# Hybrid decoder trunk on one core: an earlier order for the RWKV stage's chunk products, inversion and small products

## The chip, the core and the metric

The kernel runs on one core of one Trainium2 chip. The time is the device time of one execution in microseconds (us). Below, PE is the TensorE's matmul engine, DVE is VectorE, ACT is ScalarE, POOL is GpSimd and SP the queue that issues the DMAs. The time of the kernel before is 2563.52 us, the median of 3 runs.

## The reference

One layer of a decoder is computed for a prompt of 1024 tokens (plus 16 learned tokens) and for 8 samples of 8 tokens, both with the same weights, all in float32. The core of it:

```python
proj = x @ lw['w_in']
hA, (C1, n1, m1) = _mlstm_mixer(...)      # 4 heads, chunkwise matrix memory
hB, S1, shift1 = _rwkv7_mixer(...)        # 16 heads of 64, delta update of a state
merged = sigmoid(gA) * hA + sigmoid(gB) * hB
x1 = _layer_norm(ALPHA * x + merged @ lw['w_out'], ...)
x2 = _layer_norm(ALPHA * x1 + conv_ffn(x1), ...)

def _rwkv7_step(S, inp):
    r, w, k, v, kk, a = inp
    sa = jnp.einsum('bhvk,bhk->bhv', S, -kk)
    S = S * w[:, :, None, :] + sa[..., None] * (kk * a)[:, :, None, :] + v[..., None] * k[:, :, None, :]
    return S, jnp.einsum('bhvk,bhk->bhv', S, r)
```

The change lies in the RWKV mixer alone. The kernel computes that recurrence in chunks of 64 tokens: within a chunk the updates of the delta rule are a triangular system, whose matrix comes from products of r, a with k, b and is inverted; between chunks a state S is carried on.

## The kernel before, in words

The kernel has two phases. Phase 1 normalises the input, runs the mLSTM mixer and then the RWKV stage (from about 410 us to 1640 us of the profile); phase 2 makes the output product, the second normalisation and the convolution feed-forward. All large products are made of three float32r products of high and low parts (`mm3`, L59), 24 matmuls to a 128-row weight block; eight units of three matmuls make one block, and below a **unit** is such a group of three (`lerp`, L305, and `tanh_gate`, L328, yield after each).

The RWKV stage (`rwkv`, L1141) works on steps 0 to 11: 3 passes over the tokens (346, 384 and 384 columns) by 4 groups u of four heads each (two blocks m of 128 rows). It is a software pipeline. In step n of its loop these things go on side by side:

- the **chain** of step n (`rwkv_chain`, L935): 18 rounds of small float32 matmuls, each needing the one before, which carry the state from chunk to chunk;
- the back part of step n-1 (`rwkv_back`, L1050);
- for step n+2 the dense products of k and r (`rwkv_k`, L672, `rwkv_r`, L693), for step n+1 those of v, and some gate products; these are the units, some 102 to a step in passes 1 and 2, and they fill the time between the chain's rounds;
- for step n+2 the "inside" work (`inner`, L1236): the **chunk products** (`rwkv_g`, L770), then on DVE the **inversion** of the triangular matrices by forward substitution (`rwkv_t`, L823; 30 pairs of DVE instructions, L837 and L839, on the tile LX), then two further products and copies that complete the inverse TT (`rwkv_mid`, L872).

Four kinds of **small products** belong to the dense work: the **rate** products in `rwkv_r` (decay and in-context rate, four matmuls into the tile gg, then two tanh on ACT, L714), the **norm** products in `rwkv_r` (sums of squares over a head; sq, the square, is made by ACT, L728), the **bonus** product (`rwkv_bonus`, L845) and the **gate** product (`gates_b`, L628).

What sets the order: PE's order is the program's own (`manual_schedule`, L1327). The order on DVE, ACT and POOL is made by the framework's scheduler. The loop at L1242 has 18 rounds to a step; in each round it issues one round of the chain, then the back part, then inside work whose due time has come (due times are fractions of a step after the step in which the inside work begins), then its share of the units. Rate and norm products stand in `rwkv_r` in program order between the units; bonus and gate pieces are put in a list and issued by `dense` (L1199) after 6 or 4 units.

The tile gg is two banks of PSUM and exists once (`gbank`, L226): rate products, chunk products and the two products of the completion (`product`, L888) all go through it, so each waits until the one before has been read out. A chunk product is read by two DVE instructions into Gd (L804), an ACT copy into A21 (L810), and two DVE instructions into Gr and Gk (L812, L813). Gd exists once: the chunk products of a step may be read into it only after LX has been taken from it for the step before (L830). `product` issues its first half and, when it is called on again or when `gbank` is, its second half; its results are copied by ACT (L908 for the first, L913 for the second).

Due times before: chunk products from 0.42 of a step on, in steps of 0.075 (0.06 in pass 0, where the samples' chunk is separate), all four or five in one run; the inversion from 0.87 on for 0.75 of a step; completion from 1.78 on. The list `share` (L1167) gives the number of gate products for steps -2, -1, 0, ..., 12.

Of the kernel before, what the change touches and what calls it, by code (L numbers as in the profile page):

```python
# [43 lines left out]
class Trunk:  # L44
# [303 lines left out]
    def lora(self, pas, w, pool):  # L348
        x = self.rs.tile([P, W], F32, name="sq")
# [278 lines left out]
    def gates_b(self, pas, j, w, pool):  # L628
# [18 lines left out]
        self.small += [(self.cfg.get("b1", 4), piece)]  # L647
# [23 lines left out]

    def rwkv_k(self, pas, j, w, pool):  # L672

        nc, i = self.nc, self.i
        m = j % 2
        st = self.st[pas, j] = {}
# [16 lines left out]
    def rwkv_r(self, pas, j, w, pool):  # L693
# [8 lines left out]
        st = self.st[pas, j]  # L702
        r, k, a, b, lw = (st[n] for n in ("r", "k", "a", "b", "lw"))
# [36 lines left out]
        n2 = r_["n2"]  # L740
        ps = self.psc.tile([P, 512], F32, name="y", bufs=2)
        for p in range(NP):
            self.mm(ps[:, 2 * p:2 * p + 2], sq[:, p * 128:(p + 1) * 128], self.const("bones2"))
        c = slice(6 * m, 6 * m + 6)
        ts(n2[:, c].rearrange("p (h n) -> p n h", h=2), ps[:, 0:6].rearrange("p (n h) -> p n h", h=2), 1e-24, None, op0=ALU.max)
# [17 lines left out]
        if m:  # L763
            self.un[pas, j // 2] = dict(n2L=n2L)
# [5 lines left out]
    def rwkv_g(self, pas, u, pool):  # L770
# [6 lines left out]
        done, total = 0, 5 if pas == 0 else 4  # L777
        for m, st in self.pairs(pas, u):
# [44 lines left out]
    def rwkv_t(self, pas, u, pool):  # L823
# [9 lines left out]
        for s in range(1, 31):  # L833
# [6 lines left out]
            if s % 2 == 0:  # L840
                yield self.cfg.get("t0", 0.87) + self.cfg.get("tw", 0.75) * s / 30
# [299 lines left out]
    def rwkv(self, steps):  # L1141
# [567 lines left out]
```

## Time and profile before

| | us |
|---|---|
| median of 3 runs (2560.59 to 2563.93) | 2563.52 |
| the profiled execution's own time | 2555.19 |
| its span, first to last instruction | 2553.4 |
| PE matmul busy in it | 2373.9 (93%) |
| DVE busy | 1546.8 (61%) |
| ACT busy | 1085.0 (42%) |
| POOL busy | 477.0 (19%) |
| mean granted clock of TensorE | 0.964 of full |

Busy shares are means over stages that differ, so the RWKV stage is read from windows of the trace (times from the span's start) and from lists of who waited for whom within it. Granted clock 1.0 is 2.4 GHz and 0.5 is 1.2 GHz. A wait is put down to the releaser that came last.

### The profile page before, as it was taken

Reading aid. Unit: us, or ns where it says so; the run is one execution under the profiler, and the core shown is the slowest. Engines: PE = TensorE matmul, PEld = TensorE weight load, DVE = VectorE, ACT = ScalarE, POOL = GpSimd, SP = SyncE. Lnnn points to the kernel's source line nnn. Section 1 sums busy time; section 2 is a strip of 40 time slices with the busy share of each in tenths; the row PEclk is TensorE's granted clock in tenths of the full one; section 3 lists DMA queues with packets and bytes.
Section 4 is the critical chain, followed back from the end, with each engine's and each line's share of the span. In section 5 each row is a group of like instructions: output and inputs, shape, how many; then the busy total and the mean of one; then the engine's idle time right before and its main releaser. Section 6 shows DMA issues by size and latency. Waiting matters only on the chain. (4 is left out here: it accounts for less than half of the span.)

```text
span 2553.4 us, 43721 instructions
## 1 busy us (share of the span) xinstructions
PE 2373.9 (93%) x16303; PEld 2139.4 (84%) x16303; DVE 1546.8 (61%) x3365; ACT 1085.0 (42%) x2453; POOL 477.0 (19%) x669
## 2 busy tenths in 40 slices
PE   6999998879899899999989999998999999999997
PEld 6787996768787788888878888887999999999996
DVE  6555536888885588765698874456433333343437
ACT  4444444335434456545645655455313222132222
POOL 5100015434553212111111212221000000000003
PEclk9999998889999899999999999989999999999999
DMA  8563534435458355557455566894111111021112
GB/s 281 158 187 93 187 114 138 152 120 176 127 164 257 108 167 162 172 180 252 140 165 160 173 208 215 277 317 167 59 34 54 38 46 50 30 63 34 50 38 81
DMA packets 212362, 356.95 MB, mean 140 GB/s; under 512 B 24610, under 2 KB 83874, under 8 KB 212151
## 3 DMA queue, kind: packets, MB, share of 16 engines
q1 hardware_dynamic: 212151, 354.17, 43.5%
q8 instruction: 128, 2.10, 0.4%
q14 instruction: 83, 0.68, 0.1%
HBM read 272.00 MB, written 82.08 MB: 139 GB/s over the span
## 5 line engine op out<-in xcount | busy, mean ns | idle before, releaser
L57 PE MATMUL d<-Xh,whi 128*128 128x384 f32 (+3 forms) x1544 | 557.5, 361 | 14.7 <-ACT sm L1137 3.9
L57 PE MATMUL d<-Xl,whi 128*128 128x384 f32 (+3 forms) x1544 | 530.8, 344 | 1.2 <-DMA Xl<-xl_d 0.8
L57 PE MATMUL d<-Xh,wlo 128*128 128x384 f32 (+3 forms) x1544 | 528.3, 342 | 0.2 <-DVE wlo L74 0.2
L57 PE MATMUL d<-X1h,whi 128*128 128x364 f32 (+2 forms) x1120 | 371.4, 332 | 4.5 <-ACT whi L90 2.8
L57 PE MATMUL d<-X1h,wlo 128*128 128x364 f32 (+2 forms) x1120 | 370.4, 331 | 0.0
L57 PE MATMUL d<-X1l,whi 128*128 128x364 f32 (+2 forms) x1120 | 370.3, 331 | 0.0
L57 PEld LDWEIGHTS d<-Xh,whi 128*128 128x128 f32 (+1 forms) x1544 | 302.3, 196 | 39.5 <-issue 8.7
L57 PEld LDWEIGHTS d<-Xl,whi 128*128 128x128 f32 (+1 forms) x1544 | 302.8, 196 | 5.7 <-DMA Xl<-xl_d 4.0
L57 PEld LDWEIGHTS d<-Xh,wlo 128*128 128x128 f32 (+1 forms) x1544 | 301.8, 195 | 2.8 <-DVE wlo L74 0.6
L73 ACT CAST whi<-raw 128x512 fp32r<-128x512 f32 (+1 forms) x255 | 157.0, 617 | 339.0 <-PE d L57 277.2
L57 PEld LDWEIGHTS d<-X1h,whi 128*128 128x128 f32 x1120 | 212.1, 189 | 9.5 <-ACT whi L90 3.4
L57 PEld LDWEIGHTS d<-X1l,whi 128*128 128x128 f32 x1120 | 211.9, 189 | 4.9
L57 PEld LDWEIGHTS d<-X1h,wlo 128*128 128x128 f32 x1120 | 212.0, 189 | 3.6 <-DMA wlo<-lo_w_out_b 0.3
L90 ACT CAST whi<-raw 128x512 fp32r<-128x512 f32 x232 | 142.9, 617 | 133.3 <-PE d L57 68.5
L74 POOL TENSOR_TENSOR wlo<-raw,whi 128x512 fp32r<-128x512 f32 x120 | 164.7, 1374 | 181.5 <-ACT whi L73 162.3
L1537 DVE TENSOR_TENSOR acc<-y,acc 128x512 f32<-128x512 f32 (+1 forms) x144 | 97.5, 686 | 166.1 <-PE y L57 166.0
L74 DVE TENSOR_TENSOR wlo<-raw,whi 128x512 fp32r<-128x512 f32 (+1 forms) x135 | 98.6, 734 | 157.6 <-ACT whi L73 156.7
L839 DVE TENSOR_TENSOR LX<-LX,tm 128x30 f32<-128x30 f32 (+4 forms) x360 | 148.0, 411 | 9.8 <-DVE tm L837 0.5
L837 DVE TENSOR_TENSOR tm<-LX 128x30 f32<-128x30 f32 (+4 forms) x360 | 138.6, 385 | 8.8
L57 PE MATMUL y<-wdh,hh 128*128 128x512 f32 x352 | 138.1, 392 | 5.0 <-DVE acc L1537 5.0
L57 PE MATMUL y<-wdl,hh 128*128 128x512 f32 x352 | 137.8, 391 | 0.0
L57 PE MATMUL y<-wdh,hl 128*128 128x512 f32 x352 | 137.6, 391 | 0.0
(363 smaller groups left out, 4175.5 us busy)
## 6 DMA issues: line engine op xcount, KB each, us to landing
raw<-in_w_up_dram SPq DMA_DIRECT2D x88, 256.0 KB, 2.8
raw<-in_wv_dram SPq DMA_DIRECT2D x48, 256.0 KB, 3.1
raw<-in_wk_b_dram SPq DMA_DIRECT2D x48, 256.0 KB, 3.9
raw<-in_wr_dram SPq DMA_DIRECT2D x48, 256.0 KB, 3.2
raw<-in_wv_b_dram SPq DMA_DIRECT2D x48, 256.0 KB, 3.4
raw<-in_wgb_dram SPq DMA_DIRECT2D x48, 256.0 KB, 3.6
raw<-in_wo_dram SPq DMA_DIRECT2D x48, 256.0 KB, 3.6
raw<-in_wga_dram SPq DMA_DIRECT2D x48, 256.0 KB, 3.3
```

Of the source, the lines that this page charges most:

```text
L57: self.nc.tensor.matmul(out, lhsT, rhs, start=start, stop=stop, skip_group_check=skip)
L73: nc.scalar.copy(hi[:, :n], src[:, u:u + n])
L74: self.lo_eng.tensor_tensor(lo[:, :n], src[:, u:u + n], hi[:, :n].bitcast(F32), op=ALU.subtract)
L90: nc.scalar.copy(hi, raw)
L837: tt(tv_, LX[:, s + 1:, s:s + 1].broadcast_to([P, m, s]), LX[:, s:s + 1, 0:s].broadcast_to([P, m, s]), op=ALU.mult)
L839: tt(LX[:, s + 1:, 0:s], LX[:, s + 1:, 0:s], tv_, op=ALU.add)
L1537: tt(acc[0:m, t, ns], ps[0:m], acc[0:m, t, ns], op=ALU.add)
```

## The change

No instruction is added or removed on any engine; all of it is order.

- Rate, norm, bonus and gate products all go into the list `small`, and the loop takes one of them from it in each round, behind the chain's round, the back part and the inside work, ahead of the units. `rwkv_r` puts its rate product there at its start and flushes it before it is needed, after five units; `lora`, `rwkv_r` and the end of a step flush what is left.
- Chunk products are due pair by pair: block m=0 at 0.22, 0.33 of a step, block m=1 at 0.46, 0.57, each as soon as its block's inputs have been issued (`able`), no longer when both have; and not before the step before has begun its inversion (the flag "begun").
- The inversion is due from 0.79 on, and the completion's parts at 1.72, 1.775, 1.83, 1.885 and 1.94, one to a round.
- `share` gives step -1 nine gate products (six before), step 1 five (six) and step 2 four (six).

```diff
@@ -348,0 +349 @@
+        self.flush()
@@ -647 +648 @@
-        self.small += [(self.cfg.get("b1", 4), piece)]
+        self.small.append(piece)
@@ -671,0 +673,5 @@
+    def flush(self, last=None):
+        while self.small and (last is None or last in self.small):
+            self.small.pop(0)()
@@ -675,0 +682,2 @@
+        if not m:
+            self.un[pas, j // 2] = {}
@@ -702,0 +711,2 @@
+        self.flush()
+        self.within = True
@@ -707,9 +717,12 @@
-        zs = self.gbank()
-        for n in range(2):
-            rows = slice(64 * n, 64 * n + 64)
-            x, ps = self.xwa[n], zs[:, n, 0:W]
-            self.mm(ps, lw[0][:, 2 * rows.start:2 * rows.start + 128], x, True, False)
-            self.mm(ps, lw[1][rows], x[rows], False, True)
-        for n, (dst, bias) in enumerate(((cw, dv(3)), (ta, dv(4)))):
-            act(dst, zs[:, n, 0:W], AF.Tanh, bias=bias, scale=0.5)
-        for _ in range(4):
+        def rates():
...
+        self.small.append(rates)
+        for _ in range(5):
@@ -716,0 +730 @@
+        self.flush(rates)
@@ -740,10 +754,13 @@
-        n2 = r_["n2"]
...
-        nc.vector.reciprocal(n2[:, c], n2[:, c])
-        if m:
-            n2L = pool.tile([P, 32], F32, name="n2L", bufs=2)
-            nc.vector.transpose(n2L, n2)
+        def norms():
...
+            if m:
+                n2L = self.un[pas, j // 2]["n2L"] = pool.tile([P, 32], F32, name="n2L", bufs=2)
+                nc.vector.transpose(n2L, n2)
+        self.small.append(norms)
@@ -763,2 +780 @@
-        if m:
-            self.un[pas, j // 2] = dict(n2L=n2L)
+        self.within = False
@@ -777,2 +793,5 @@
-        done, total = 0, 5 if pas == 0 else 4
-        for m, st in self.pairs(pas, u):
+        for m in range(2):
+            un["wait"] = "DL", m
+            yield 0.22 + 0.24 * m
+            done, total = 0, 3 if pas == 0 else 2
+            st = self.st[pas, 2 * u + m]
@@ -815 +834,2 @@
-                    yield self.cfg.get("g0", 0.42) + self.cfg.get("gw", 0.3) * done / total
+                    yield 0.22 + 0.24 * m + 0.22 * done / total
+        un["wait"] = "n2L", None
@@ -829 +849 @@
-        yield self.cfg.get("t0", 0.87)
+        yield self.cfg.get("t0", 0.79)
@@ -830,0 +851 @@
+        self.un[pas, u]["begun"] = True
@@ -843 +864 @@
-        yield self.cfg.get("t0", 0.87) + self.cfg.get("tw", 0.75)
+        yield self.cfg.get("t0", 0.79) + self.cfg.get("tw", 0.75)
@@ -869 +890 @@
-        self.small += [(6, piece)]
+        self.small.append(piece)
@@ -879 +900 @@
-        m0 = self.cfg.get("m0", 1.78) if (pas, u) != (0, 0) else self.cfg.get("m00", 1.78)
+        m0 = self.cfg.get("m0", 1.72) if (pas, u) != (0, 0) else self.cfg.get("m00", 1.72)
@@ -885 +906 @@
-        yield m0 + 0.1
+        yield m0 + 0.055
@@ -908 +929 @@
-        yield from (m0 + 0.12 for _ in product(A21, Tn, 0, 32, lambda w, h1: nc.scalar.copy(P1[h1], w[h1])))
+        yield from (m0 + 0.11 for _ in product(A21, Tn, 0, 32, lambda w, h1: nc.scalar.copy(P1[h1], w[h1])))
@@ -912,2 +933,2 @@
-        yield m0 + 0.15
-        yield from (m0 + 0.17 for _ in product(P1, Tx, 32, 0, lambda w, h0: nc.scalar.copy(
+        yield m0 + 0.165
+        yield from (m0 + 0.22 for _ in product(P1, Tx, 32, 0, lambda w, h0: nc.scalar.copy(
@@ -917 +938 @@
-            yield m0 + 0.2
+            yield m0 + 0.23
@@ -1143 +1164 @@
-        self.st, self.un, self.tho, self.mt, self.rest = {}, {}, {}, {}, None
+        self.st, self.un, self.tho, self.mt, self.rest, self.small, self.within = {}, {}, {}, {}, None, [], False
@@ -1167 +1188 @@
-        share = self.cfg.get("ga", [0] + [6] * 8 + [5, 5, 5, 9, 0, 0])
+        share = self.cfg.get("ga", [0, 9, 6, 5, 4, 6, 6, 6, 6, 5, 5, 5, 9, 0, 0])
@@ -1201,2 +1221,0 @@
-            since = 0
-            self.small = []
@@ -1211,2 +1230 @@
-                    while self.small:
-                        self.small.pop(0)[1]()
+                    self.flush()
@@ -1218,2 +1235,0 @@
-                if not self.small:
-                    since = 0
@@ -1225,6 +1241 @@
-                    since += 1
-                    if self.small and since >= self.small[0][0]:
-                        self.small.pop(0)[1]()
-                        since = 0
-            while self.small:
-                self.small.pop(0)[1]()
+            self.flush()
@@ -1239,0 +1251,7 @@
+        def able(m):
+            pas, u = steps[m]
+            what, which = self.un.get((pas, u), {}).get("wait", ("DL", 0))
+            where = self.un.get((pas, u), ()) if which is None else self.st.get((pas, 2 * u + which), ())
+            return what in where and (m == 0 or "begun" in self.un[steps[m - 1]])
@@ -1246 +1264 @@
-                inside[n + 2] = [0.42, inner(n + 2)]
+                inside[n + 2] = [0.22, inner(n + 2)]
@@ -1256 +1274 @@
-                if r == 12 and 0 <= n + 1 < N:
+                if r >= 12 and 0 <= n + 1 < N and "bon" not in self.st[steps[n + 1][0], 2 * steps[n + 1][1]] and not self.within:
@@ -1264 +1282 @@
-                    while x[0] <= now and "n2L" in self.un.get(steps[m], ()):
+                    while x[0] <= now and able(m):
@@ -1266 +1284 @@
-                        if m in starts and x[0] < self.cfg.get("t0", 0.87):
+                        if m in starts and x[0] < self.cfg.get("t0", 0.79):
@@ -1267,0 +1286,2 @@
+                if self.small:
+                    self.small.pop(0)()
```

What the order becomes, at three places.

PE, in the last rounds of step 8, where products that complete an inverse are issued (T is the inverse so far, A the matrix A21, d the dense products, u, y and t the chain's; a product is issued in two halves). Before, the second half of the first product and the first half of the second follow each other:

```order
L57 MATMUL d<-Xh,wlo 128x384
L57 MATMUL u<-VU,KBT 64x64 x4
L57 MATMUL y<-VU,Gr 64x64 x4
L57 MATMUL gg<-T_16352,A_14800 32x32 x12
L57 MATMUL gg<-T_16350,A_14800 32x32 x12
L57 MATMUL d<-Xh,whi 128x384
```

In the change each half stands in a round of its own, here one half of the second product:

```order
L57 MATMUL d<-Xh,wlo 128x384
L57 MATMUL u<-Rs,TT_4224 64x64 x4
L973 MATMUL t<-cst,v 128x128
L975 MATMUL t<-cst,KB 128x128 x2
L57 MATMUL gg<-T_16241,A_14812 32x32 x12
L57 MATMUL d<-Xh,whi 128x384
```

The two products that stood side by side on gg are now a round of dense units apart.

DVE, step 8: the last products of k and b (KB), then the reading of the first chunk product for step 10 (Gd, Gr, Gk), with n the norms and T the transposed inverse. Before:

```order
L759 TENSOR_TENSOR KB<-KB,ta 128x3x2x64
L1039 SCALAR_TENSOR_TENSOR S_4211<-u,DL,SD 64x64 x4
L1083 SCALAR_TENSOR_TENSOR ysq<-t,pt,bon 128x3x64 x2
L882 STREAM_TRANSPOSE T_16350<-LX 128x1024
L884 STREAM_TRANSPOSE T_16352<-LX 128x1024
L760 TENSOR_TENSOR KB<-KB,sm 128x3x128
L804 TENSOR_TENSOR Gd<-gg,cst 32x6x32 x2
L1083 SCALAR_TENSOR_TENSOR ysq<-t,pt,bon 128x3x64 x2
L323 SCALAR_TENSOR_TENSOR v<-d,pd,sm 128x384
L1092 SCALAR_TENSOR_TENSOR ysq<-ysq,pt,mA 128x384
L812 TENSOR_TENSOR Gr<-gg,cst 128x384
L813 TENSOR_TENSOR Gk<-gg,cst 64x384
```

The change:

```order
L777 TENSOR_TENSOR KB<-KB,sm 128x3x2x64
L860 TENSOR_TENSOR LX<-LX,tm 128x2x29
L858 TENSOR_TENSOR tm<-LX 128x30
L860 TENSOR_TENSOR LX<-LX,tm 128x30
L863 TENSOR_TENSOR LX<-LX,n2L 128x1024
L823 TENSOR_TENSOR Gd<-gg,cst 32x6x32 x2
L903 STREAM_TRANSPOSE T_16241<-LX 128x1024
L905 STREAM_TRANSPOSE T_16243<-LX 128x1024
L760 TENSOR_SCALAR n_4231<-y 128x3x2
L831 TENSOR_TENSOR Gr<-gg,cst 128x384
L832 TENSOR_TENSOR Gk<-gg,cst 64x384
```

Before, the two transposes of LX were over when the first chunk product was read, and that reading came many rows after the products of block m=0; now the last product of block m=0, the end of the inversion and the two transposes stand directly around it.

ACT, step 8: sq and the rates' two tanh (cw, ta). Before:

```order
L321 ACTIVATE sm<-d,pt 128x384
L714 ACTIVATE cw<-gg,pd 128x384
L714 ACTIVATE ta<-gg,pd 128x384
L728 ACTIVATE sq<-KB,pt 128x3x64 x2
L1041 COPY Yt<-y 128x128
```

The change:

```order
L321 ACTIVATE sm<-d,pt 128x384
L742 ACTIVATE sq<-KB,pt 128x3x64 x2
L1062 COPY Yt<-y 128x128
L998 ACTIVATE SD<-S_4211,DL 128x128
L725 ACTIVATE cw<-gg,pd 128x384
L725 ACTIVATE ta<-gg,pd 128x384
```

The squares now stand ahead of the two tanh instead of behind them.

## Rows read from the trace of the kernel before

**Rows 1.** Busy time by stretch: us, PE, PEld, DVE, ACT, POOL busy, clock, DMA share, GB/s.
```profile
440.00:551.00 111.00, 83.12 (x576) 75.06 (x574) 96.69 (x221) 39.12 (x87) 47.40 (x61) 0.83 0.45 141
551.00:755.00 204.00, 180.43 (x1546) 157.84 (x1545) 170.49 (x378) 99.04 (x252) 103.10 (x127) 0.95 0.50 155
755.00:971.00 216.00, 199.07 (x1549) 172.95 (x1548) 146.44 (x321) 105.31 (x259) 49.65 (x81) 0.92 0.55 173
971.00:1339.00 368.00, 348.62 (x2931) 306.37 (x2930) 272.82 (x659) 206.28 (x505) 54.82 (x96) 0.98 0.56 180
1339.00:1640.00 301.00, 289.60 (x2522) 255.87 (x2521) 198.72 (x481) 171.88 (x439) 62.59 (x65) 0.98 0.63 197
```

**Rows 2.** Waits of PE, 440 to 1640, then 440 to 551: total, times, longest.
```profile
PE gg L57 <- DVE Gk L813: 28.3, 15, 3.9
PE gg L57 <- DVE T L884: 17.0, 3, 14.3
PE gg L57 <- ACT A L908: 12.7, 12, 1.1
PE y L57 <- ACT sq L728: 9.9, 2, 5.2
PE y L57 <- POOL T L929: 5.8, 3, 2.8
...
PE gg L57 <- DVE Gk L813: 10.2, 7, 3.0
```

**Rows 3.** Timeline of PE completing one inverse: start, us, [idle before <-releaser].
```profile
1418.01 0.85 PE L57 MATMUL gg<-T,A 32*32 32x32 f32 x24 [1.05 <-ACT A L908]
```

**Rows 4.** Groups of instructions, ACT, the copies behind the second product: busy, mean ns.
```profile
L913 ACT COPY TT<-gg 32x384 f32<-32x384 f32 x24 | 20.1, 837 | 1.0 <-PE gg L57 0.9
```

**Rows 5.** Timeline of ACT, step 0, the squares.
```profile
582.55 0.80 ACT L728 ACTIVATE sq<-KB,pt 128x192 f32<-128x192 f32 x2 [2.66 <-DVE KB L323]
```

**Rows 6.** Timeline of PE, then of DVE, at the first step's inverse.
```profile
525.59 0.87 PE L57 MATMUL gg<-T,A 32*32 32x32 f32 x24 [14.31 <-DVE T L884]
...
523.65 1.89 DVE L884 STREAM_TRANSPOSE T<-LX 128x1024 f32<-128x1024 f32 x1
```

**Rows 7.** Groups of DVE, the reading of chunk products: busy, mean ns.
```profile
L804 DVE TENSOR_TENSOR Gd<-gg,cst 32x192 f32<-32x192 f32 x80 | 40.1, 502 | 16.4 <-PE gg L57 15.2
...
L813 DVE TENSOR_TENSOR Gk<-gg,cst 64x384 f32<-64x384 f32 x40 | 22.0, 549 | 0.3
```

**Rows 8.** Timelines of PE and DVE, step 9, then step 1: rates to last KB product.
```profile
1428.35 0.70 PE L57 MATMUL gg<-xw,lw 128*128 128x384 f32 x2
...
1435.92 0.83 PE L57 MATMUL y<-cst,sq 128*128 128x2 f32 x6
...
1438.38 0.76 PE L57 MATMUL u<-Rs,TT 64*64 64x64 f32 x8
...
1439.04 0.56 DVE L760 TENSOR_TENSOR KB<-KB,sm 128x384 f32<-128x384 f32 x1
...
654.07 0.71 PE L57 MATMUL gg<-xw,lw 128*128 128x384 f32 x2
...
680.71 0.51 DVE L760 TENSOR_TENSOR KB<-KB,sm 128x384 f32<-128x384 f32 x1
```

**Rows 9.** Timeline of PE, dense matmuls of 346 columns at either clock.
```profile
470.33 0.32 PE L57 MATMUL d<-Xl,whi 128*128 128x346 f32 x1
...
470.49 0.33 PE L57 MATMUL d<-Xh,wlo 128*128 128x346 f32 x1
...
485.91 0.49 PE L57 MATMUL d<-Xh,whi 128*128 128x346 f32 x1
...
486.20 0.49 PE L57 MATMUL d<-Xl,whi 128*128 128x346 f32 x1
```

**Rows 10.** Timeline of DVE, then of POOL, step 9.
```profile
1428.36 1.51 DVE L839 TENSOR_TENSOR LX<-LX,tm 128x184 f32<-128x184 f32 x1
...
1428.13 1.53 POOL L1074 TENSOR_TENSOR Yt<-Yt,yvar 128x768 f32<-128x768 f32 x1
```

More of the change, by code (lines that the diff above doesn't have):

```diff
@@ L705, in rwkv_r @@
         units = self.lerp(pas, w, j, mu(0), dv(0), r, pool)
-        zs = self.gbank()
-        for n in range(2):
-            rows = slice(64 * n, 64 * n + 64)
-            x, ps = self.xwa[n], zs[:, n, 0:W]
-            self.mm(ps, lw[0][:, 2 * rows.start:2 * rows.start + 128], x, True, False)
-            self.mm(ps, lw[1][rows], x[rows], False, True)
-        for n, (dst, bias) in enumerate(((cw, dv(3)), (ta, dv(4)))):
-            act(dst, zs[:, n, 0:W], AF.Tanh, bias=bias, scale=0.5)
-        for _ in range(4):
+        def rates():
+            zs = self.gbank()
+            for n in range(2):
+                rows = slice(64 * n, 64 * n + 64)
+                x, ps = self.xwa[n], zs[:, n, 0:W]
+                self.mm(ps, lw[0][:, 2 * rows.start:2 * rows.start + 128], x, True, False)
+                self.mm(ps, lw[1][rows], x[rows], False, True)
+            for n, (dst, bias) in enumerate(((cw, dv(3)), (ta, dv(4)))):
+                act(dst, zs[:, n, 0:W], AF.Tanh, bias=bias, scale=0.5)
+        self.small.append(rates)
+        for _ in range(5):
             yield next(units)
+        self.flush(rates)
         ts(cw, cw, DECAY_C, DECAY_C, op0=ALU.mult, op1=ALU.add)
@@ L738, in rwkv_r @@
         yield from units
-        n2 = r_["n2"]
[L741 to L745, printed above, removed]
-        nc.vector.reciprocal(n2[:, c], n2[:, c])
-        if m:
-            n2L = pool.tile([P, 32], F32, name="n2L", bufs=2)
-            nc.vector.transpose(n2L, n2)
+        def norms():
+            n2 = r_["n2"]
+            ps = self.psc.tile([P, 512], F32, name="y", bufs=2)
+            for p in range(NP):
+                self.mm(ps[:, 2 * p:2 * p + 2], sq[:, p * 128:(p + 1) * 128], self.const("bones2"))
+            c = slice(6 * m, 6 * m + 6)
+            ts(n2[:, c].rearrange("p (h n) -> p n h", h=2), ps[:, 0:6].rearrange("p (n h) -> p n h", h=2), 1e-24, None, op0=ALU.max)
+            nc.vector.reciprocal(n2[:, c], n2[:, c])
+            if m:
+                n2L = self.un[pas, j // 2]["n2L"] = pool.tile([P, 32], F32, name="n2L", bufs=2)
+                nc.vector.transpose(n2L, n2)
+        self.small.append(norms)
         yield
@@ L840, in rwkv_t @@
             if s % 2 == 0:
-                yield self.cfg.get("t0", 0.87) + self.cfg.get("tw", 0.75) * s / 30
+                yield self.cfg.get("t0", 0.79) + self.cfg.get("tw", 0.75) * s / 30
         tt(LX, LX, n2L.unsqueeze(1).broadcast_to([P, 32, 32]), op=ALU.mult)
-        yield self.cfg.get("t0", 0.87) + self.cfg.get("tw", 0.75)
+        yield self.cfg.get("t0", 0.79) + self.cfg.get("tw", 0.75)
     def rwkv_bonus(self, pas, j, pool):
```

## The prediction

> **What bounds the kernel now.** I first read the windows of the RWKV stage [rows 1]. In every stretch from 440 to 1640 us PE is busy far more than any other engine, except in the first, 440 to 551, where PE has 83.1 of 111 us and DVE 96.7. Summed over the five rows PE is busy 1100.8 of 1200 us, so 99 us are idle. The granted clock adds to that: 1 minus the clock, times the length, times two is the time spent at 1.2 GHz: 38, 20, 35, 15 and 12 us, 119 in all, idle time included. What a us at the low level loses is seen in two pairs of equal matmuls, which start 0.16 us apart at one level and 0.29 at the other [rows 9]: 45%. So the stage has two stores from which a new order can draw: idle PE time, and a clock that falls where PE idles (0.92 and 0.95 in the two stretches of pass 0, 0.98 where PE idles about 5%).
>
> Next come the waits of PE [rows 2]. They name gg above all: 28.3 us behind the last reading of a chunk product (15 waits, 10.2 us of it in the seven before 551), 17.0 behind the transposed inverse (one wait of 14.3), 12.7 behind the copy of a product of the completion (12 waits, each about 1.05 [rows 3]), 9.9 behind the squares, 5.8 behind a transpose on POOL in pass 0 (L929). No instruction is added or removed, so all that can change is these waits, new ones like them, and the clock.
>
> **The change part by part.** All terms are us of the profiled execution, 2555.19, which is 8.3 under the median of the runs.
>
> *Completion, spread over rounds.* A copy of 1.05 now lies behind a round's units instead of on the path [rows 3]. Ten of the twelve waits go: -10.5. In two steps (2 and 6, where a pass ends) the order puts the next rates right behind the second product; they then wait for the two copies behind it, 2 x 0.84 [rows 4], in place of nothing: +1.8. Sum -8.7.
>
> *Norm products, a round or more later, and squares ahead of the tanh on ACT.* The two waits over 4 us and what is with them go: -9.9 [rows 2]. A doubt: in step 0 the square itself waited 2.66 us for DVE's KB [rows 5], so a part may stay if DVE is later still.
>
> *POOL's transpose.* The product before it ends some three units earlier. A unit is three matmuls at 0.16, 0.48 [rows 9]; 3 x 0.48 = 1.45 for each of three waits, of which two are longer than that and the third is short: -3.3 of 5.8.
>
> *The first inverse.* PE waits 14.31 us for a transpose that DVE ends at 525.5 [rows 6]; DVE is the bound there [rows 1]. The same instructions stand ahead of it in both orders, so the chunk products of step 1, of which five now come in a run, wait under the same cover and cost nothing by themselves; if the cover were gone they would cost their readings, about 3.5 each. Readings that come in between on DVE push the transposes to between 527 and 533; I take 4 us. The order has 17 more units behind the inverse and ahead of the chain's start (17 x 0.48 = +8.2) and 24 fewer later, in steps 1 and 2 (-11.5), since step -1 got three gate products more. Sum +0.7.
>
> *Readings of chunk products.* Outside the start 28.3 - 10.2 = 18.1 us of waits stand behind them [rows 2]. In most steps each product on gg is now followed by a round of other work, longer than its reading of about 2 x 0.50 + 2 x 0.55 us on DVE [rows 7]. They all go, -18.1, and three new costs are put against them:
>
> 1. **Chunk products wait for their inputs.** In steps 0, 1, 4, 5, 8 and 9 the first product of block m=0 now comes soon after that block's k and b have been made. Between the rates and this product PE has, by the order, the rates (0.70 [rows 8]), about eight units (24 matmuls of 384 columns, 0.18 each by scaling 0.16 from 346: 4.3), the norms (0.83) and two pieces of the chain (about 0.8 to 1.2 each): some 8 us. Before, the last KB of a block was written 11.25 us after its rates began in step 9 (to 1439.6), and 27.1 us after them in step 1 (to 681.2) [rows 8]. From above: 4 x 3.2 in passes 1 and 2, 2 x 18 in pass 0: 49. From below: 0, since the order puts less in between on DVE (in step 8 the k product now directly precedes the inversion's end). I take 2.5 each, nearer the row of step 9, six times: +15.
> 2. **Rates behind chunk products.** In steps 4 and 8 two transposes, 1.89 for the one in [rows 6], now stand between a product's readings. That makes about 5.5 us against some 4.7 of PE's work: 0.7, four times: +2.8.
> 3. **Two products in one round** in steps 3 and 7: the second waits a reading, about 3: +6.
>
> With these the readings come out at +5.7.
>
> As to two products in a row on the one tile, the Trainium skill (Perfetto Trace Analysis, section Optimizing Tensor Performance, Matmuls) says that independent matmul groups should go round different PSUM banks so that the read-out of one overlaps the next; gg is two banks that are used as one, and [rows 2] agree with 28.3 us. By that rule the change would gain wherever it parts such products and pay only in steps 3 and 7 and at the start.
>
> *Clock.* The low level followed waits of some us on PE [rows 1, 2]. With the two waits of about 5 us and some of about 3 gone I take 9 us fewer at 1.2 GHz: 9 x 0.45 = -4. Bounds: 0, and -17 if the 55 us of 551 to 971 came down to the 17 that a clock of 0.98 would make.
>
> **Sum:** -8.7 - 9.9 - 3.3 + 0.7 + 5.7 - 4 = -19.5. The profiled execution would take 2535.7, the median **2544**. About 0.2% (5.1 us) is what a measurement of this kernel can tell from no change.
>
> **The rivals.**
>
> *DVE delivers late (slower).* The place is the first chunk product of block m=0 in the six steps of item 1. DVE is busy 170 of 204 us in steps 0 and 1 [rows 1], and one of its instructions of some 0.4 us took 1.51, beginning 0.2 us after a POOL instruction of 1.53 and ending with it [rows 10]. If such meetings, or the inversion that is now due sooner, keep the last KB as late as it was before, item 1 is at its upper end, 49 instead of 15: 2544 + 34 = **2578**. It decides from 15 + 19.5 = 34.5 us over the six waits, 5.8 each. For it speaks step 1's 27 us; against it that only steps 0 and 1 are so crowded, and that POOL has under 63 us busy in each of the later stretches. A rule of the Trainium skill speaks for it (SBUF - State Buffer, section Who interferes with whom): a DVE instruction with two inputs in SBUF contends with a GpSimd instruction that reads SBUF, and the one that comes second is held off; [rows 10] agree, and the KB products have both inputs there.
>
> *Waits only move (no change).* In pass 0 DVE sets the pace, and what PE gains there it waits for at the next product. Then the norms' 9.9, POOL's 3.3 and the clock's 4 are not gained: -2.3, a median of **2561**. For it speaks the square that itself waited for DVE [rows 5].
>
> *Everything arrives in time (faster still).* Item 1 costs nothing (-15), and the clock gives half of its bound, 8.5 instead of 4 (-4.5): **2524**. Against it stand step 1's 27 us.
>
> That the change moves nothing is excluded by the order itself.
>
> **How the numbers follow.** Forecast 0.45; DVE late 0.22; waits move 0.18; all in time 0.15. The forecast's own bounds (item 1 by 10 either way, the clock by 4) reach from 2533 to 2556. The range leaves out about the outer half of the two extreme rivals: 2514 to 2578. Faster by over 0.2% are the forecast, all in time: 0.60. Waits move lies within 0.2%, less a little that belongs to slower: 0.17. Slower: 0.23.
>
> **What would show it.** Right: PE's waits behind the copy of the first product (A, now L929) fall from 12.7 us to about 3; no wait over 1 us behind the squares; few waits of gg behind Gk (now L832) between 551 and 1640, except one in each of steps 3 and 7; the first wait behind the inverse ends between 527 and 533, and the chain's first step begins some 10 us later than 551 without the end of the stage being later. Item 1 shows as waits of gg behind KB (L777, L778) of about 2.5. The forecast is wrong if these are over 5.8 each, if DVE's busy share in pass 0 is unchanged and PE idles there under other names, or if the clock of 551 to 971 falls below 0.92.

## The result, and the profile after

The change is **slower**: 2592.83 us, the median of 4 runs (2589.52 to 2603.86), against 2563.72 for the kernel before beside it. The ratio is 1.0116, 95% interval 1.0087 to 1.0145. Run again beside other kernels it was 1.0128 (1.0097 to 1.0159). The forecast was 2544, range 2514 to 2578.

The profiled execution took 2603.86 us (span 2601.8), 48.7 more than that of before and itself 11 above its median, so the first thing is to see where those 48.7 us lie. The RWKV stage, taken from the first rate product to the end of the last product with an inverse in a chain (u from Rs and TT), took 1212.3 us before and 1243.3 now: +31. It began 10.1 us later (423.0 after 412.9), and 7.6 us were added behind it. Those two parts belong to the execution more than to the change: in a second profile of the same kernel the stage began at 414.9, and in the profiles of the other kernels below it began anywhere from 411.5 to 425.5. So the 31 us are what has to be explained.

Windows of the change by the same stretches of the program (each ends where the chain of the same step begins; the last ends as far behind the last chain as in [rows 1]). Columns as in [rows 1]:

```profile
440.00:576.00 136.00, 106.44 (x693) 97.77 (x693) 113.01 (x262) 49.80 (x113) 63.45 (x79) 0.82 0.48 155
576.00:781.00 205.00, 183.54 (x1529) 158.89 (x1526) 165.60 (x356) 96.88 (x247) 95.28 (x119) 0.91 0.46 145
781.00:992.00 211.00, 182.93 (x1487) 157.43 (x1485) 151.07 (x337) 101.42 (x249) 45.09 (x79) 0.93 0.52 167
992.00:1376.00 384.00, 356.52 (x2929) 312.87 (x2929) 272.87 (x657) 206.96 (x505) 55.45 (x97) 0.95 0.53 171
1376.00:1681.00 305.00, 294.67 (x2528) 260.99 (x2528) 197.56 (x469) 172.51 (x439) 60.99 (x66) 0.97 0.61 195
```

Against [rows 1] the first stretch is 25 us longer, 10 of them because the stage began later. It has 117 matmuls more, 72 of them the 24 units that the new shares put there. The next two stretches have 79 matmuls fewer and are together only 4 us shorter; the fourth, with the same matmuls but two, is 16 longer. The granted clock is lower in steps 0 and 1 (0.91 after 0.95) and in passes 1 and 2 (0.95 and 0.97 after 0.98). The whole stage, before and in the change:

```profile
412.90:1625.21 1212.31, 1112.63 (x9147) 977.18 (x9147) 895.45 (x2085) 628.75 (x1551) 336.57 (x472) 0.95 0.55 174
...
423.04:1666.30 1243.26, 1126.52 (x9141) 988.75 (x9141) 904.54 (x2085) 629.02 (x1550) 333.24 (x472) 0.93 0.53 169
```

PE's idle time rose from 99.7 to 116.7 us, and the matmuls that started at 1.2 GHz from 463 to 611; PE's busy time is 13.9 us longer for the same instructions but six. 17.0 + 13.9 are the 31 us. How much of the 13.9 is the change's own is less sure than the sum looks: a kernel as fast as the one before (d2 below) had 6 us more PE busy time in its profile than the profile of before. That the clock fell doesn't hang on these profiles: the median granted clock of whole runs was 0.954 in both sets of runs of the change, and 0.962 in the 23 runs of the kernel before beside the second set.

The waits of PE, 440 to 1640 us of the change (total, times, longest):

```profile
PE gg L57 <- DVE T L905: 25.0, 3, 11.4
PE gg L57 <- DVE Gk L832: 19.1, 9, 4.7
PE gg L57 <- DVE KB L777: 18.9, 6, 4.4
PE gg L57 <- DVE S L1054: 10.3, 3, 4.0
PE gg L57 <- DVE T L1035: 7.5, 3, 4.8
PE gg L57 <- DVE LX L860: 6.7, 2, 4.5
PE gg L57 <- DVE tm L858: 4.6, 1, 4.6
PE gg L57 <- ACT TT L934: 3.6, 2, 1.9
...
PE y L57 <- ACT sq L742: 2.0, 1, 2.0
```

The old names are nearly gone, as was forecast: the product's copy (12.7 in [rows 2]) has no row and its successor 3.6, the squares 2.0 after 9.9, POOL's transpose none after 5.8, Gk outside the start about 4.7 after 18.1. New ones stand in their place: KB, the samples' state S and its transposes (L1054, L1035), and T. The waits of 4.6 and 4.5 us behind tm and LX are the second of two chunk products in one round, in steps 3 and 7: DVE ended the reading of the first one (Gk, L832) within 0.2 us of the instructions named.

Three places show how they arise. PE, then DVE, in step 0:

```profile
589.43 1.27 PE L57 MATMUL gg<-xw,lw 128*128 128x384 f32 x2 [4.05 <-DVE S L1054]
...
604.92 0.80 PE L57 MATMUL gg<-RA,KB 64*128 64x128 f32 x4 [4.33 <-DVE KB L777]
...
590.58 1.95 DVE L905 STREAM_TRANSPOSE T<-LX 128x1024 f32<-128x1024 f32 x1
...
603.71 0.56 DVE L776 TENSOR_TENSOR KB<-KB,ta 128x384 f32<-128x384 f32 x1
604.30 0.56 DVE L777 TENSOR_TENSOR KB<-KB,sm 128x384 f32<-128x384 f32 x1
```

The rates of block m=0 wait 4.05 us for the samples' reading. From their start at 589.43 it is 15.4 us until the last KB product ends at 604.86, with the transposes of the previous inverse in between; PE has 11.2 us of other work and stands still for 4.33. The chunk product is in PE's queue ahead of dense units that need nothing from DVE. The same holds at steps 1, 5, 8 and 9 (3.87, 4.40, 2.07, 4.05); at step 4 the wait is 0.19.

PE at the inverses with which passes 1 and 2 begin:

```profile
970.05 0.87 PE L57 MATMUL gg<-T,A 32*32 32x32 f32 x24 [11.41 <-DVE T L905]
...
1354.29 0.87 PE L57 MATMUL gg<-T,A 32*32 32x32 f32 x24 [9.73 <-DVE T L905]
```

Before, the first of these waited 0.2 us and the second 2.5. Counted in the order, between the last chunk product of step 4 and the first product with its inverse there stood 65 dense units; now 43: the last chunk product comes ten units later, the product with the inverse twelve earlier. For step 8 it was 60 and is 40. DVE took 54 to 56 us for the inversions of steps 0, 4 and 8 before, and 48 to 52 now. Step 0 had 55 units there and has 38. Its inversion begins at 494.7 after 471.3; 10.1 of these 23 us are the later start of the stage, and 13.3 come from the order, which brings the last chunk product of step 0 later. DVE of the kernel before:

```profile
471.27 1.25 DVE L830 STREAM_TRANSPOSE LX<-Gd 128x1024 f32<-128x1024 f32 x1
```

DVE, then PE, of the change:

```profile
494.72 1.25 DVE L850 STREAM_TRANSPOSE LX<-Gd 128x1024 f32<-128x1024 f32 x1
...
542.70 0.87 PE L57 MATMUL gg<-T,A 32*32 32x32 f32 x24 [3.84 <-DVE T L905]
```

### The profile page after: what moved, and what is told of

Read it like the earlier page. It is cut to its first block, busy times and chain, and to the rows that moved or that the text cites. A ratio compares the mean times of both kernels' runs of the same rounds, so it can differ in the third digit from the quotient of the medians.

```text
span 2601.8 us, 43754 instructions
## 1 busy us (share of the span) xinstructions
PE 2400.4 (92%) x16303; PEld 2160.0 (83%) x16303; DVE 1554.9 (60%) x3365; ACT 1085.1 (42%) x2453; POOL 473.3 (18%) x669
## 4 chain that ended last, share of the span: by engine, by line
PE 58%; DVE 15%; DMA 6%; ACT 3%; issue 2%; POOL 0%; SPq 0%; DVEq 0%; ACTq 0%; POOLq 0%
PE d L57 38%; PE y L57 13%; PE gg L57 4%; DVE tm L858 2%; DVE LX L860 2%; PE u L57 2%; DVE Gd L823 1%; DVE S L1060 1%; DMA mA<-gA_d 1%; DVE acc L125 1%; DMA raw<-in_w_out_b_dram 1%; DMA tho<-mA_d 1%; DVE tho L626 1%; DMA mg_d<-mA 1%; DVE T L905 0%
## 5 line engine op out<-in xcount | busy, mean ns | idle before, releaser
L57 PE MATMUL d<-X1h,wlo 128*128 128x364 f32 (+3 forms) x1120 | 370.9, 331 | 0.0
L57 PE MATMUL d<-X1l,whi 128*128 128x364 f32 (+3 forms) x1120 | 370.3, 331 | 0.0
L57 PEld LDWEIGHTS d<-X1h,whi 128*128 128x128 f32 x1120 | 212.2, 190 | 10.4 <-ACT whi L90 2.8
L858 DVE TENSOR_TENSOR tm<-LX 128x30 f32<-128x30 f32 (+4 forms) x360 | 148.5, 412 | 9.7
L860 DVE TENSOR_TENSOR LX<-LX,tm 128x30 f32<-128x30 f32 (+4 forms) x360 | 138.2, 384 | 10.4 <-DVE tm L858 0.5
```

The source lines that it names most:

```text
L57: self.nc.tensor.matmul(out, lhsT, rhs, start=start, stop=stop, skip_group_check=skip)
L858: tt(tv_, LX[:, s + 1:, s:s + 1].broadcast_to([P, m, s]), LX[:, s:s + 1, 0:s].broadcast_to([P, m, s]), op=ALU.mult)
L860: tt(LX[:, s + 1:, 0:s], LX[:, s + 1:, 0:s], tv_, op=ALU.add)
```

## The experiments

All times are ratios to the kernel before, run beside them, with 95% intervals; 0.001 is 2.6 us. **Theory 1** was that PE asks for the first inverse of a pass too early. **Theory 2** was that the chunk products are asked for before their inputs are there.

**a0_change_again.** The change, no edit.

> The change itself once more, as the level from which the next three are read. Both theories expect 1.009 to 1.014 of the kernel before, and PE's three long waits behind the transposed inverse (3.8, 11.4 and 9.7 us in the first profile) within 2 us of these.

1.0128 (1.0097 to 1.0159), profiled execution 2591.02. The three waits behind T were 5.85, 10.87 and 9.76 us, 26.5 in all; KB 18.6 in five. The picture holds.

**a1_first_inverses.**

```diff
-            yield 0.22 + 0.24 * m
+            yield 0.22 + 0.24 * m if u else -1.0
...
-        m0 = self.cfg.get("m0", 1.72) if (pas, u) != (0, 0) else self.cfg.get("m00", 1.72)
+        m0 = 1.72 if u else 1.78
+        d1, d2, d3, d4, d5 = (0.055, 0.11, 0.165, 0.22, 0.23) if u else (0.1, 0.12, 0.15, 0.17, 0.2)
...
```

Here d1 to d5 are the spacing of the completion's parts, the old one for the steps that begin a pass (u = 0); and the chunk products of these steps lose no round at the start of a block.

> The change, but the steps that begin a pass (0, 4, 8) have their completion due as before (from 1.78 on, in its old spacing), and their chunk products lose no round at the start of a block. Theory 1 (PE reaches the completion of a pass's first inverse before DVE has it): the waits behind T, 25.0 us in the change's profile, fall under 4, and the time falls by 20 to 30 us, to 1.000 to 1.004 of the kernel before. Theory 2 (chunk products asked for before DVE has their inputs): the T waits are given back at the next product on gg, the time falls by less than 8 us and stays above 1.008.

1.0118 (1.0088 to 1.0148): no gain that can be told. No wait of PE behind T of 1 us or more is left, but others took its place:

```profile
PE gg L57 <- DVE Gk L832: 38.9, 13, 5.6
PE gg L57 <- DVE KB L777: 23.6, 6, 6.0
```

Gk rose from 18.4 (a0) to 38.9, KB from 18.6 to 23.6. The edit itself is a likely reason: six of the waits behind Gk, 23.8 us together, stand in steps 3 and 7, where the chunk products of a first step now meet the rates. What the old due time alone is worth was not run, so theory 1 is left to the next kernel.

**a2_products_late.**

```diff
-            yield 0.22 + 0.24 * m
+            yield 0.42 + 0.16 * m
...
-                    yield 0.22 + 0.24 * m + 0.22 * done / total
+                    yield 0.42 + 0.16 * m + 0.16 * done / total
...
```

> The change, but the chunk products are due from 0.42 (block m=0) and 0.58 (m=1) of a step on, 0.08 apart (0.05 in pass 0), instead of 0.22 and 0.46. Theory 2: the waits of chunk products behind KB (18.7 us in five) and of rates behind the samples' reading S (10.3) go, the clock of pass 0 rises, and the time falls by 20 to 30 us, to 1.000 to 1.004 of the kernel before. Theory 1: the T waits stay at about 25 us and the time falls by 0 to 10 us.

0.9985 (0.9966 to 1.0005): 37 us less than the change, as theory 2 had it and somewhat more. KB is no longer among PE's waits, though T waits longer (38.7) and S waits as before (10.1):

```profile
PE gg L57 <- DVE T L905: 38.7, 3, 14.2
PE gg L57 <- DVE Gk L832: 24.7, 13, 4.7
PE gg L57 <- DVE S L1054: 10.1, 3, 4.0
```

So theory 1 falls as the main cause: the waits for T are longer than in the change, and the time is that of before. The whole stage, of a0 and then of a2:

```profile
414.90:1656.74 1241.84, 1127.50 (x9141) 988.66 (x9141) 905.58 (x2085) 628.36 (x1550) 333.69 (x472) 0.92 0.54 170
...
423.93:1633.78 1209.85, 1105.87 (x9141) 971.90 (x9141) 901.55 (x2085) 627.03 (x1550) 338.60 (x472) 0.94 0.55 174
```

Of the 32 us between them 10.4 are idle time of PE and 21.6 are PE's busy time for the same matmuls. By these two profiles two thirds of what the early products cost is not the waits themselves, but matmuls at the lower clock.

Step 5 shows what one wait is worth. Windows from chain start to chain start, first of a0, then of a2:

```profile
1076.20:1166.80 90.60, 86.29 (x727) 76.52 (x728) 66.98 (x163) 50.28 (x125) 12.53 (x24) 0.96 0.53 169
```

```profile
1065.90:1150.40 84.50, 83.55 (x727) 73.93 (x728) 66.85 (x165) 49.94 (x125) 13.26 (x25) 1.00 0.58 182
```

The same 727 matmuls: PE idles 4.3 us in the one (a wait behind KB of 4.31) and 1.0 in the other, and is busy 2.7 us longer at a clock of 0.96 instead of 1.00. The wait of 4.3 us made the step 6.1 longer.

**a3_both.** Both edits.

> Both edits of the two kernels before. If the causes are separate, the sum of the two gains; theory 1 alone: as the first inverses alone, within 6 us; theory 2 alone: as the late products alone, within 6 us. If both hold with some 20 us each, 0.992 to 0.998 of the kernel before.

0.9957 (0.9935 to 0.9979): against the late products alone, 0.9985, 6 to 7 us better, at the edge of what the intervals can tell. With the products in their place the first inverses may matter a little.

**b0_products_mid.**

```diff
-            yield 0.22 + 0.24 * m
+            yield 0.30 + 0.22 * m
...
-                    yield 0.22 + 0.24 * m + 0.22 * done / total
+                    yield 0.30 + 0.22 * m + 0.20 * done / total
...
```

> The change, but the chunk products are due from 0.30 (block m=0) and 0.52 (m=1) of a step on: about 20 dense units after the block's rates instead of 9, where the late kernel has 30. Theory 2a (the products stand ahead of their inputs): the waits behind KB shrink under 1 us each, and the time comes within 10 us of the late kernel, 0.996 to 1.002 of the kernel before. Theory 2b (what costs is that they stand between the rates and norms on the one tile gg, and that their readings push the products of k and r aside on DVE): a half-way place, 1.004 to 1.010.

1.0004 (0.9985 to 1.0022), 5 us from the late kernel and some 30 from the change. No wait behind KB is left, though the bonus products wait 9.4 us for Dt (3.4 in the change). Eleven units more between a block's rates and its chunk product are enough: theory 2a.

**b1_early_products_alone.** The kernel before, with

```diff
-        for m, st in self.pairs(pas, u):
+        for m in range(2):
+            un["wait"] = ("DL", m) if u else ("n2L", None)
+            yield 0.22 + 0.24 * m if u else -1.0
...
-                while x[0] <= now and "n2L" in self.un.get(steps[m], ()):
+                while x[0] <= now and able(m):
```

> The kernel before with one part of the change alone: chunk products due from 0.22 and 0.46, each when its own block's inputs have been issued, for all steps that don't begin a pass. Theory 2: five or six waits of gg behind KB of 3 to 6 us each appear, and it is slower than before by 15 to 35 us, 1.006 to 1.014. If the early products hurt only together with the small products in the rounds: within 0.4% of before.

1.0105 (1.0081 to 1.0129). One part makes as much as the whole change. PE, steps 0 and 1:

```profile
579.70 0.80 PE L57 MATMUL gg<-RA,KB 64*128 64x128 f32 x4 [6.32 <-DVE KB L762]
...
684.43 0.80 PE L57 MATMUL gg<-RA,KB 64*128 64x128 f32 x4 [6.39 <-DVE KB L762]
```

KB makes 17.6 us in five waits (6.3 and 6.4 here, then 2.1, 0.7 and 2.1 in passes 1 and 2). The 4.68 and 5.18 us behind the squares in these steps are gone, though norms were not moved: one backlog of DVE is waited for at the earlier place. And the chain waits for its own state behind DVE's readings (S, L1046: 9.1 us in nine waits, under 2 before). The whole stage:

```profile
422.96:1658.41 1235.45, 1126.98 (x9147) 987.85 (x9147) 893.15 (x2085) 628.80 (x1552) 334.67 (x472) 0.93 0.54 171
```

Against the kernel before PE is idle 8.8 us more and busy 14.4 us more for the same matmuls: the split is that of a0 and a2.

**b2_small_products_alone.** The change with its other parts put back: chunk products from 0.42 on in one run, t0 0.87, m0 1.78, old spacing, old shares.

> The kernel before with rate, norm, bonus and gate products in the list that the rounds serve, all else (chunk products, inversion, completion, shares) as before. By the prediction's terms: the waits behind the squares (9.9 us) go, and most of those of rates behind Gk; a wait for the samples' reading may come; 5 to 20 us faster, 0.992 to 0.998. Rival: the rates now meet the chunk products of the step that ends a pass, and it is within 0.2% of before.

1.0043 (1.0023 to 1.0064): slower, neither the gain nor the rival's no change. PE, rate products:

```profile
577.88 1.27 PE L57 MATMUL gg<-xw,lw 128*128 128x384 f32 x2 [3.91 <-DVE S L1051]
...
676.86 1.27 PE L57 MATMUL gg<-xw,lw 128*128 128x384 f32 x2 [4.19 <-DVE S L1051]
...
886.53 1.27 PE L57 MATMUL gg<-xw,lw 128*128 128x384 f32 x2 [3.75 <-DVE Gk L829]
...
908.35 0.92 PE L57 MATMUL gg<-xw,lw 128*128 128x384 f32 x2 [3.56 <-DVE Gk L829]
```

In a round the small product stands right behind the inside work, so at the ends of passes a rate meets a chunk product in the same round (3.75, 3.56, and 3.00, 3.88 in step 7), and in pass 0 the samples' state. Rates waited 9.1 us in all before; here 28.1.

**b3_spread_completion_alone.** The kernel before, completion at 1.72, 1.775, 1.83, 1.885, 1.94 for u > 0.

> The kernel before with the completion spread over five rounds from 1.72 on, in the steps that don't begin a pass. By the prediction's term nine waits of 1.05 us behind the first product's copy go, but the rates at the ends of the two first passes wait for the second product's copies: 6 to 9 us faster, 0.9965 to 0.998. Rival: the copy's wait only moves, within 3 us of before.

0.9954 (0.9934 to 0.9973), 12 us, more than the 6 to 9 of the term. The waits behind the copy are down to three. Those behind POOL's transpose are gone, but the samples' products now wait for DVE's transposes instead (L1015, 4.6 us):

```profile
PE gg L57 <- DVE T L1015: 4.6, 3, 1.9
PE gg L57 <- ACT TT L914: 3.5, 2, 1.8
PE gg L57 <- ACT A L909: 3.2, 3, 1.1
```

**c0_rates_in_place.** As b2, but

```diff
-        self.small.append(rates)
-        for _ in range(5):
+        rates()
+        for _ in range(4):
...
```

> The kernel before with norm, bonus and gate products in the rounds' list, but the rate products where they were, at the start of rwkv_r between the units. Theory: what made the small products alone slower were the rates, which in the rounds meet a chunk product on gg at the start and in the steps that end a pass (waits of 3.0 to 3.9 us there) and the samples' reading in pass 0 (3.9, 4.2); without them the waits behind the squares (9.9 us) are gained: 0.995 to 0.998 of the kernel before. Rival: the norms or the gate pieces cost as much in the rounds as they gain: 1.000 or above.

0.9985 (0.9964 to 1.0006), between theory and rival: the rates were what made b2 slower (-15 us), but the 9.9 us of the squares show as some 4, which the interval doesn't tell from nothing. The waits behind the squares are gone; others are longer or new (behind Rs 3.5 us after 2.1, behind KB 2.6 and LX 2.4 after none).

**c1_rates_in_place_spread.** With b3's completion too.

> The same with the completion spread over five rounds in the steps that don't begin a pass. If the two gains add up: 0.990 to 0.994. If the squares' waits and the spread completion draw on the same idle time in pass 0: 0.994 to 0.997.

0.9974 (0.9962 to 0.9986): outside both ranges, and no better than b3 alone. Norms, bonus and gates in the rounds are worth nothing here.

**c2_and_share.** With the change's `share` too.

> The same with the change's shares of gate products (step -1 nine, step 1 five, step 2 four). The last chunk product of step 0 stands 10 units later (73 after 63), its inverse is asked for 22 units later (140 after 118): by that the first wait for T, 14.5 us, falls by some 12 units less what DVE starts later, to 7 to 10, and the time by 3 to 6 us against the kernel before it in this call. Rival: T comes later by as much as PE does, the wait stays above 13 us, and it is 0 to 6 us slower.

0.9882 (0.986 to 0.9904), 23 us (0.92%) better than c1, where 3 to 6 were expected, and with d3 below the **fastest kernel of all**, ahead of both that were compared. The first wait for T fell from 13.7 to 11.3 only, not to 7 to 10. Yet the start, from the first rate product to the first product with an inverse in the chain, took only 1.4 us longer (143.6, then 145.0) with 24 units more in it, and step 2, from which 16 were taken, is 17 us shorter at the full clock. Windows of step 2, of c1, then of c2:

```profile
757.10:863.20 106.10, 97.32 (x752) 82.71 (x752) 63.39 (x128) 51.79 (x131) 41.84 (x57) 0.92 0.64 203
```

```profile
747.20:836.20 89.00, 83.16 (x700) 69.46 (x701) 63.56 (x128) 48.16 (x122) 33.60 (x49) 1.00 0.64 207
```

**c3_both_small_first.** a3, with the two lines `if self.small: self.small.pop(0)()` ahead of the inside work of a round.

> The kernel with both edits (late products, first inverses as before), but in a round the small product is issued ahead of the inside work. Theory: a rate product behind a chunk product waits for five readings on DVE and ACT (2.6 to 4.3 us in the steps that end a pass), a chunk product behind a rate product only for two tanh on ACT (about 1.3); four to six waits lose 2 us each: 0.991 to 0.994 of the kernel before, where it was 0.9957. Rival: the chunk products become later and with them the first inverse of the pass: no gain, 0.995 to 0.998.

0.9917 (0.9896 to 0.9939): 10 us better than a3. Rates behind a chunk product are replaced by chunk products behind two tanh (ta, L725), 1.14 us each. PE's waits behind Gk were 36.7 us in sixteen in a3; now:

```profile
PE gg L57 <- DVE Gk L832: 15.1, 13, 4.2
...
PE gg L57 <- ACT ta L725: 7.2, 6, 1.4
```

**d0_share_alone.** The kernel before with the change's `share`.

> The kernel before with the change's shares of gate products alone. If the gain of 29 us that the shares gave on top of the spread completion stands by itself (24 units done under the first wait for T, a shorter step 1 and 2, their clock up): 0.988 to 0.993. If it needed the other edits: 0.996 to 1.000.

0.9906 (0.9882 to 0.993). The gain stands by itself.

**d1_change_old_share.** The change with the `share` of before.

> The change with the shares of before. If the shares are worth as much inside the change: 20 to 30 us slower than the change, 1.018 to 1.024 of the kernel before. If their gain is used up there, because the change's order leaves fewer units between the last chunk product of step 0 and its inverse (38, with the old shares 31, before 55): within 8 us of the change, 1.009 to 1.016.

1.0102 (1.0081 to 1.0123). Inside the change the shares gain nothing. Windows from 440 us to the chain of step 0 and on to that of step 3. The kernel before, then d0:

```profile
440.00:551.10 111.10, 83.22 (x576) 75.17 (x575) 96.69 (x221) 39.16 (x88) 47.40 (x61) 0.83 0.45 141
551.10:857.40 306.30, 274.91 (x2293) 239.61 (x2294) 229.16 (x494) 150.75 (x381) 140.58 (x182) 0.95 0.55 171
```

```profile
440.00:557.70 117.70, 95.04 (x661) 86.66 (x661) 104.95 (x228) 45.70 (x103) 58.65 (x73) 0.87 0.53 169
557.70:840.70 283.00, 264.17 (x2218) 228.20 (x2219) 223.62 (x490) 143.15 (x367) 134.38 (x172) 0.95 0.55 172
```

d1, then the change (a0):

```profile
440.00:554.00 114.00, 80.70 (x575) 72.90 (x573) 98.32 (x227) 39.26 (x86) 45.30 (x60) 0.82 0.43 136
554.00:867.30 313.30, 282.39 (x2293) 242.96 (x2294) 227.84 (x486) 149.67 (x381) 141.65 (x180) 0.92 0.53 167
```

```profile
440.00:569.40 129.40, 99.99 (x665) 91.30 (x664) 108.53 (x244) 45.09 (x104) 57.67 (x72) 0.83 0.48 153
569.40:868.80 299.40, 269.27 (x2218) 230.40 (x2218) 223.56 (x473) 144.88 (x367) 128.78 (x171) 0.92 0.51 162
```

In both pairs the shares shorten steps 0 to 2 (by 23.3 and 13.9 us) and lengthen the start, by 6.6 in the old order and 15.4 in the change's. The stage itself began 2.2 and 2.5 us later in the second of each pair (412.9 and 415.1, 412.4 and 414.9); without that the start is longer by 4.4 and 12.9, and the sums are -18.9 against -1.0.

The order differs as the second theory had it. In the old one 12 of the 24 units stand between step 0's last chunk product and its inverse (55 units, then 67), 10 ahead of that product and 2 behind the inverse. In the change 12 stand ahead of it, where they make the inversion start later, 5 behind the inverse, and only 7 (31, then 38) in between. But this explains a part at most. PE's idle time in the start falls by about as much in both pairs (27.9 to 22.7, 33.3 to 29.4). What tells them apart is PE's busy time in the start, +11.8 and +19.3 for 85 and 90 matmuls more, at clocks of 0.87 and 0.83, and PE's idle time in steps 0 to 2: 31.4 to 18.8 in the old order, 30.9 to 30.1 in the change's. In the old order the waits behind the squares fall from 9.9 to 5.6 us and those behind POOL's transpose from 5.8 to 2.0; the change has the waits behind KB and S in their place, which stay at 28.7 us in d1 and 28.9 in a0 (all over the stage). Why these don't shrink was not tested.

**d2_inversion_early_alone.** The kernel before with t0 = 0.79.

> The kernel before with the inversion due from 0.79 alone. No step waits for an inverse but those that begin a pass, and there the due time is long past when the chunk products are read: 0.998 to 1.002. Rival: DVE takes inversion rows ahead of the products of k and r, and PE waits for these: above 1.002.

1.0002 (0.9983 to 1.0022): nothing.

**d3_spread_and_share.** b3 with the change's `share`.

> The kernel before with the spread completion and the shares of gate products, rate and norm products as before. If the two gains add up: 0.984 to 0.990, as good as or better than the kernel that also had norms, bonus and gates in the list (0.9882). If norms in the list are needed for the shares' gain: 0.991 to 0.996.

0.9888 (0.9862 to 0.9914), as good as c2: the list in the rounds isn't needed. The two gains together, 1.12%, are less than their sum, 1.40%.

The parts alone: early chunk products +1.05%, small products +0.43, spread completion -0.46, earlier inversion 0, shares -0.94. The first four add up to 1.04% (the inversion measured +0.02), and the change without its shares measured 1.02%. What is over in the change itself, 0.14 to 0.26% by its two comparisons, is within what a comparison here can tell. The agreement is closer than the parts allow: b1 and b3 leave the steps that begin a pass as they were.

## Why the prediction was wrong

The steps that failed are **item 1 of the readings of chunk products, which charged an early product with its wait and nothing else, and the term of the clock, which was given a gain**. The runs show +1.05% (27 us) for the early products alone (b1) where item 1 had 15 us, and a clock that fell: 13.9 us more PE busy time in the change's stage where the term had -4. In the change's profile the waits that went come to 9.1 (copies) + 7.9 (squares) + 5.8 (POOL) + 13.4 (Gk outside the start) = 36.2, near the 40.0 of the terms. Those that came are KB 18.9, S 7.5 more, its transposes 7.5, two products in a round 9.1, T 8.0 more and Gk in the start 4.0: 55.0, where the terms had 24.5. With the clock's 13.9 that is +32.7 for the 31 measured (the waits left out here are small ones, and PE's idle time as a whole rose by 17.0, not 18.8). Term by term:

- *Completion* (-8.7): right in mechanism. The copies' 12.7 us became 3.6; alone the edit gave -12 (b3). POOL's transposes, forecast at -3.3 of 5.8, are no longer waited for, but DVE's transposes of the samples are: 4.6 us in b3, 7.5 in the change.
- *Norm products* (-9.9): the waits fell as forecast, the time didn't (c0, c1). The doubt that was noted at [rows 5] fits what c0 shows: the square waited for DVE's backlog, and PE now meets a backlog at the next things that it wants from DVE and ACT. b1 shows it the other way round. That is the rival "waits only move", for this term alone.
- *Chunk products wait for their inputs* (+15): 18.9 us in the trace, so the size of the waits was nearly right. The upper end of 49 was not reached, since the last KB product came 15.4 and 14.1 us after the rates in steps 0 and 1 of the change, where step 1 had 27.1 before [rows 8]. The step that failed is that nothing but the wait was charged. In b1 the same edit cost 27 us, and in the two pairs that hold the edit apart most of the cost is PE's busy time at a lower clock: 8.8 us idle and 14.4 busy (before, b1), 10.4 and 21.6 (a2, a0).
- *Clock* (-4): the sign was wrong, +13.9. The prediction counted the old waits of 3 to 5 us that would go, and not its own new ones as waits of the same kind, though item 1 had priced them. By step 5 of a0 and a2, a wait of 4.3 us cost 6.1.
- *Rates behind chunk products* (+2.8): the order was read for two transposes in steps 4 and 8, and what stood ahead of the rates on gg in pass 0 was missed. They waited 10.3 us for the samples' state (2.8 before, by a chunk product). *Two products in one round* (+6): 4.60 and 4.51, against about 3 each.
- *The first inverse* (+0.7): the time of T was right, by another way than the one given. Counted from the start of the stage T ended at 112.6 us before and at 119.6 in the change (120.6 in a0): 7 to 8 us later, about the upper end of the 1.5 to 7.5 that 527 to 533 meant. "The same instructions stand ahead of it in both orders" was true, but "DVE is the bound there" does not describe it: PE's order brought the last chunk product later, so that DVE began the inversion 13.3 us later, and the inversion itself took 47.9 us instead of 54.3. The shares were counted as 24 units that pay themselves back. Inside the change they do, and no more (-1.0 us by the windows of d1 and a0); in the old order they are worth -0.94% (d0).
- *Nothing for T at the ends of passes*: it was 21 us in the profile, the cover having shrunk from 65 and 60 units to 43 and 40. By a2, where the waits for T are 38.7 us and the time is that of before, these are not what the change lost by; with the products late, the edit of a1 is worth 6 to 7.

The rival that called it slower named the right place, the first chunk product of block m=0, but its condition, 34.5 us over six waits, was not met (18.9); what it left out, the clock, the samples' state and T, made up the rest. As to the rule that it leaned on (the Trainium skill, SBUF - State Buffer, section Who interferes with whom), the measured case needs no contention: in all six places the last three KB products ran in 0.52 to 0.56 us each. What made them late in step 0 were two transposes ahead of them and inputs that came late: between 595.6 and 603.1 us DVE stood idle for 4.2 us, 2.34 of them behind ACT's Dt.

## What to carry over

On PE, whose order is the program's own, an instruction moved up makes everything queued behind it wait with it: before it is issued earlier, compare the engine's own work up to that place with the time at which its input lands, at each step of the pipeline, and charge the wait twice, for itself and for the clock. What spare work is worth depends on the order around it (here 24 us in one order and nothing in the other), so count the units between what starts a long off-engine job and what wants its result, before and after, and then measure. Measure the parts of a bundled change alone: here two parts gained 0.5 and 0.9%, and the bundle lost 1.2.

## What was not expected of the hardware

A short wait of PE went with a low clock that lasted longer than the wait: in step 5, with one wait of 4.31 us, the granted clock was 0.96 over 90.6 us, which is 7 us at 1.2 GHz, and 727 matmuls took 86.3 us instead of 83.6 at 1.00. And the change's own stage began at 423.0 us in one profile and at 414.9 in the other, so that only the medians of several runs carry a difference of half a per cent.
